# Seven-product matrix multiplication: another order of the seven products, and another split of the weight sums between transfer and VectorE

## The chip, the cores and the metric

The kernel runs on one core of one Trainium2 chip. The metric is the device time of one execution in microseconds (us). In the rows PE is TensorE's matmul, PEld its weight load, DVE is VectorE, ACT is ScalarE, POOL is GpSimd, and SP (SPq) is the queue of SyncE, which issues most of the transfers (DMA). An instruction runs on its engine in the order in which the program lists it; engines wait for one another by semaphores.

## The reference, cut to what matters

The reference is one block of a diffusion model on 512 tokens of width 2048: a mixer (a state-space scan beside a long convolution), then a SwiGLU feed-forward layer of width 5632, all in float32. The change touches the feed-forward layer alone:

```python
def swiglu(h, wg, wu, wd):
    return (jax.nn.silu(h @ wg) * (h @ wu)) @ wd
...
        x = x + g2 * rmsnorm(swiglu(h, w_gate[layer], w_up[layer], w_down[layer]), norm_ffn_post[layer])
```

## The kernel before, in words

**Arithmetic.** Each float32 operand is held as a rounded high part and a low part (`whi`, `wlo` for weights; `fh`, `fl` and `th`, `tl` for activations), and a product is three matmuls: high by high (line 1433), high weight by low activation (1435), low weight by high activation (1436).

**Groups and places.** Most of the feed-forward layer is done in 54 groups (`quad(q)`), 38 of `w_gate` and `w_up` in turn (even numbers are `w_gate`), then 16 of `w_down`. A group multiplies a 2 by 2 arrangement of weight blocks W11, W12, W21, W22 (`r11`, `r12`, `r21`, `r22`, each 128x1024, 512 KB, all named `rq` in the rows) by a 2 by 2 arrangement of activation blocks with seven block products instead of eight (Winograd's form of Strassen's method). Below, a *place* is the position of a product in its group, 1 to 7; the code counts `i` from 0. A place is 8 steps of three matmuls of 256 columns. Of the seven weight operands four are sums of blocks: W21+W22 is always made by a transfer that adds into its destination (`accum_op=ADD`, issued by POOL) during the group before; of the others, before, W11+W21 is made by such a transfer within the group, into `r11`, and the two that build on it, W11+W21+W22 in `r22` and the sum of all four in `r12`, by DVE. The activation operands (blocks in `fh`/`fl`, sums in `th`/`tl`) stay in place for 38 groups, and are replaced twice, at groups 38 and 46, when `w_down` needs the next part of the hidden layer (`replace`): transfers from `hd` into `tl` and `fl`, then a cast on ACT (line 1368) and a subtraction on DVE (1370) for each.

**What sets the order.** `feed(raw, body)` is called once for each place, in order. It issues the cast of the high part on ACT (1347) and, one call later, the subtraction for the low part on DVE (line 80, by `pend`); the matmuls of a place are issued two calls after its own. `late` holds a group's result sums, `hooks` the actions of a numbered call (`at(n, ...)`): the transfers and splits of `replace`, and `sums`, which makes the sums `T` of a finished hidden block. Instructions of one engine may be moved past each other by a scheduler before the program is fixed, except DMA issues and the splits of `replace`, which are pinned. The result `R` of a group collects the products from four accumulators in PSUM (`acc`, one bank each, two products in most). `ada(1)` is a piece of another, small computation: it loads a 512 KB block into the buffer `T` (`rt<-in_ada`) and adds it into `ada` with two DVE operations (line 77), in `w_gate` groups and in some of `w_down`. `KICKS` splits one matmul of a group in two narrower ones, at a place that runs through a cycle of six groups; the rows below use these split matmuls, which show as `x2`, as marks of a place.

Of the kernel before, what the change touches and what calls it, by code (L numbers as in the profile page):

```python
# [65 lines left out]
def block_kernel(ctx: ExitStack, tc: tile.TileContext, I: dict, out: bass.AP, dbg=None, stop=None):  # L66
    nc = tc.nc
# [1259 lines left out]
    def place(j, k, area):  # L1327
        if j == 0:
            return [f[:, area : area + 256] for f in fx[k]]
        if j in (1, 6):  # L1330
            o = 0 if j == 1 else 256
            return [f[:, o : o + 256] for f in fx[k + 8]]
        b = {2: 3, 3: 0, 4: 2, 5: 1}[j]
        return [t[:, b, :] for t in tx[k]]

    SRC = {0: 0, 1: 2, 6: 3, 3: 4, 5: 5, 4: 6, 2: 7}
# [35 lines left out]
    def replace(q, c, area):  # L1372

        n = 7 * (q - 1)
        for j, load, first in ((1, 4, 6), (6, 9, 11)):
            for k in range(8):
                d = place(j, k, 0)
                at(n + load, lambda d=d, k=k, j=j: op_load(d, hd[CH[c][k]][:, SRC[j], :]))
                at(n + first + k // 2, lambda d=d: op_split(d))
        for o, loads, first in ((2, (7, 5), 9), (0, (6, 8), 10)):  # L1380
            for k in range(8):
                for e in range(2):
                    d = [t[:, o + e, :] for t in tx[k]]
                    at(n + loads[e], lambda d=d, k=k, e=e, o=o: op_load(d, hd[CH[c][k]][:, 4 + o + e, :]))
                d = [t[:, o : o + 2, :] for t in tx[k]]
                at(n + first + k // 4, lambda d=d: op_split(d))
        for k in range(8):
            d = place(0, k, area)
            at(7 * (q - 4) + k, lambda d=d, k=k: op_load(d, hd[CH[c][k]][:, 0, :]))
            at(7 * (q - 4) + k + 2, lambda d=d: op_split(d))  # L1390
# [22 lines left out]
    nxt = [qload(t, quads[0][0][i, j]) for t, i, j in (("ra", 0, 0), ("ra", 0, 1), ("raw", 1, 0), ("raw", 1, 1))]  # L1413
    dma(nxt[2], quads[0][0][1, 1], nc.gpsimd, accum_op=ADD)

    def quad(q):
# [5 lines left out]
        def body(i):  # L1422
            def run(w):
                if i in (0, 2, 3, 5):
                    ps[i] = acc()
                b, o = {0: (0, 0), 1: (0, 1), 2: (2, 1), 3: (3, 1), 4: (3, 0), 5: (5, 0), 6: (2, 0)}[i]
# [17 lines left out]
        def early():  # L1444
            p12, p75, p6 = ps[0], ps[3], ps[5]
            nc.scalar.copy(out=R[:, 0, :], in_=p12[:, 0:256])
            tt(nc.vector, R[:, 0, :], p6[:, 0:256], R[:, 0, :], SUB)
            tt(nc.vector, R[:, 2, :], R[:, 0, :], p75[:, 0:256], SUB)
            tt(nc.vector, R[:, 1:4:2, :], R[:, 0:4:2, :], p75[:, 256:512].unsqueeze(1).broadcast_to([128, 2, 256]), ADD)
            nc.scalar.copy(out=R[:, 0, :], in_=p12[:, 0:256])  # L1450
            tt(nc.vector, R[:, 0, :], R[:, 0, :], p12[:, 256:512], ADD)

        def end():

            tt(nc.vector, R[:, 1, :], ps[2][:, 0:256], R[:, 1, :], SUB)
            tt(nc.vector, R[:, 2, :], R[:, 2, :], ps[2][:, 256:512], SUB)
# [21 lines left out]
        nsrc = quads[q + 1][0] if more else None  # L1478
        n11 = qload("ra", nsrc[0, 0] if more else I["w_dc"][2])
        feed(r11, body(0))  # L1480
        n12 = qload("ra", nsrc[0, 1] if more else I["w_dc"][3])
        n21 = qload("raw", nsrc[1, 0] if more else I["w_dc"][0])
        feed(r12, body(1))
        dma(r11, src[1, 0], nc.gpsimd, accum_op=ADD)
        if more:
            dma(n21, nsrc[1, 1], nc.gpsimd, accum_op=ADD)
        feed(r22, body(2))
        feed(r21, body(3))
        feed(r11, body(4))
        if kind != "w_up" and q < NG + 10:  # L1490
            ada(1)
        tt(nc.vector, r22, r22, r11, ADD)
        n22 = qload("raw", nsrc[1, 1] if more else I["w_dc"][1])
        feed(r22, body(5))
        tt(nc.vector, r12, r12, r22, ADD)
        feed(r12, body(6))
# [279 lines left out]
```

## Time and profile before

| | before |
|---|---|
| median of 3 runs | 2528.96 us (2522.35 to 2530.49) |
| the profiled execution | 2524.72 us, of which its span is 2523.0 us |
| granted TensorE clock, mean over the span | 0.975 |
| PE busy | 2390.1 us (95% of the span) |
| DVE busy | 1888.3 us (75%) |
| ACT busy | 972.0 us (39%) |
| POOL busy | 558.9 us (22%) |

The page of the profile gives busy time by engine, the chain of waits that ended last, and groups of like instructions. Since matmuls overlap in their pipeline, a busy PE is not a PE at its best pace; the pace is read from start to start of marked matmuls. The groups run from 1274.19 us to about 2366 us of the span. Times in rows are us from the start of the span.

### The profile page before, as it was taken

How to read it: one execution, taken by the hardware profiler on the slowest of the kernel's cores; microseconds unless marked ns; L12 is line 12 of the kernel's file. 1: busy time of each engine (PE TensorE's matmuls, PEld its weight loads, DVE VectorE, ACT ScalarE, POOL GpSimd, SP SyncE). 2: the span in 40 equal slices, each digit the busy share in tenths (PEclk: the TensorE clock that was granted, in tenths of full speed). 3: DMA queues.
4: the chain of work that ended last, by engine and by line, in shares of the span. 5: the costliest groups of instructions: out<-in, count | busy, mean ns of one | idle time of the engine just before them, and what ended most of it. 6: DMA issues, size and time to landing. Idle time of an engine off the chain costs nothing.

```text
span 2523.0 us, 41024 instructions
## 1 busy us (share of the span) xinstructions
PE 2390.1 (95%) x16138; PEld 2125.1 (84%) x16138; DVE 1888.3 (75%) x2478; ACT 972.0 (39%) x1351; POOL 558.9 (22%) x537
## 2 busy tenths in 40 slices
PE   8999999899899999998999999999999989999996
PEld 3467879677666788998999999999999989989986
DVE  7986756788878866688967777777777788677546
ACT  3143325222123412455434444444444454444334
POOL 1230010466523334653010000000000000000105
PEclk9999999999899999999999999999999989989998
DMA  7867754444455575646677676767777788777853
GB/s 290 304 228 243 236 170 157 158 134 159 146 186 185 186 283 177 208 142 194 192 208 205 193 210 194 192 193 200 218 203 194 218 243 237 225 204 196 247 179 127
DMA packets 183593, 508.72 MB, mean 202 GB/s; under 512 B 19455, under 2 KB 65471, under 8 KB 181864
## 3 DMA queue, kind: packets, MB, share of 16 engines
q1 hardware_dynamic: 166696, 445.27, 52.1%
q0 software_dynamic: 16704, 60.82, 13.7%
q8 instruction: 127, 2.08, 0.3%
q14 instruction: 66, 0.54, 0.1%
HBM read 454.12 MB, written 51.90 MB: 201 GB/s over the span
## 4 chain that ended last, share of the span: by engine, by line
PE 42%; DVE 6%; DMA 5%; issue 2%; ACT 1%; POOL 1%; SPq 0%; POOLq 0%; DVEq 0%; ACTq 0%
PE acc L1433 12%; PE acc L1436 12%; PE acc L1435 12%; PE acc L83 5%; DVE wlo L80 2%; DMA rq<-in_w_up 2%; DMA rq<-in_w_gate 1%; DVE y L80 1%; DMA fl<-hd 1%; DMA tl<-hd 1%; DVE tb L80 0%; POOL gs L80 0%; DMA hd<-sg 0%; DMA raw<-in_w_up 0%; ACT whi L1347 0%
## 5 line engine op out<-in xcount | busy, mean ns | idle before, releaser
L1347 ACT CAST whi<-rq 128x1024 fp32r<-128x1024 f32 x378 | 397.3, 1051 | 568.7 <-PE acc L1435 442.9
L80 DVE TENSOR_TENSOR wlo<-rq,whi 128x1024 fp32r<-128x1024 f32 x382 | 464.6, 1222 | 150.5 <-ACT whi L1347 144.8
L1433 PE MATMUL acc<-th,whi 128*128 128x256 f32 (+1 forms) x1755 | 486.3, 280 | 13.0 <-ACT th L1368 9.6
L1436 PE MATMUL acc<-th,wlo 128*128 128x256 f32 x1728 | 484.3, 280 | 11.6 <-DVE wlo L80 11.6
L1435 PE MATMUL acc<-tl,whi 128*128 128x256 f32 x1728 | 485.4, 281 | 2.0 <-DVE tl L1370 1.4
L179 ACT CAST whi<-raw 128x1024 fp32r<-128x1024 f32 (+1 forms) x216 | 221.5, 1026 | 481.6 <-PE acc L83 276.1
L1433 PE MATMUL acc<-fh,whi 128*128 128x256 f32 (+1 forms) x1323 | 361.5, 276 | 1.9 <-ACT whi L1347 1.3
L1435 PE MATMUL acc<-fl,whi 128*128 128x256 f32 x1296 | 359.2, 277 | 0.0
L1436 PE MATMUL acc<-fh,wlo 128*128 128x256 f32 x1296 | 358.7, 277 | 0.0
L80 DVE TENSOR_TENSOR wlo<-raw,whi 128x1024 fp32r<-128x1024 f32 x200 | 260.7, 1303 | 123.6 <-ACT whi L179 119.9
L1433 PEld LDWEIGHTS acc<-th,whi 128*128 128x128 f32 x1755 | 332.3, 191 | 14.8 <-ACT th L1368 13.1
L1436 PEld LDWEIGHTS acc<-th,wlo 128*128 128x128 f32 x1728 | 329.4, 191 | 13.7 <-DVE wlo L80 13.5
L1435 PEld LDWEIGHTS acc<-tl,whi 128*128 128x128 f32 x1728 | 329.8, 191 | 4.4 <-DVE tl L1370 4.3
L83 PE MATMUL acc<-hh,whi 128*128 128x512 f32 x688 | 285.1, 416 | 3.9 <-ACT hh L74 3.7
L83 PE MATMUL acc<-hl,whi 128*128 128x512 f32 x688 | 277.4, 403 | 3.6 <-DVE hl L77 3.6
L83 PE MATMUL acc<-hh,wlo 128*128 128x512 f32 x688 | 276.6, 402 | 0.0
L1433 PEld LDWEIGHTS acc<-fh,whi 128*128 128x128 f32 x1323 | 246.4, 188 | 2.6 <-ACT whi L1347 1.5
L1435 PEld LDWEIGHTS acc<-fl,whi 128*128 128x128 f32 x1296 | 244.0, 188 | 0.0
L1436 PEld LDWEIGHTS acc<-fh,wlo 128*128 128x128 f32 x1296 | 243.4, 188 | 0.0
L77 DVE SCALAR_TENSOR_TENSOR ada<-raw,cc,ada 128x512 f32<-128x512 f32 x198 | 169.5, 856 | 42.1 <-DMA raw<-in_ada 39.6
L80 DVE TENSOR_TENSOR rq<-rq,rq 128x1024 f32<-128x1024 f32 x108 | 132.1, 1223 | 66.2 <-DMA rq<-in_w_up 42.2
L83 PEld LDWEIGHTS acc<-hh,whi 128*128 128x128 f32 x688 | 134.3, 196 | 39.6 <-issue 5.6
(333 smaller groups left out, 4523.7 us busy)
## 6 DMA issues: line engine op xcount, KB each, us to landing
raw<-in_ada SPq DMA_DIRECT2D x106, 512.0 KB, 4.0
rq<-in_w_gate SPq DMA_DIRECT2D x76, 512.0 KB, 5.7
rq<-in_w_up SPq DMA_DIRECT2D x76, 512.0 KB, 4.3
ada<-in_ada SPq DMA_DIRECT2D x64, 512.0 KB, 4.7
rq<-in_w_ds SPq DMA_DIRECT2D x64, 512.0 KB, 4.3
raw<-in_w_hy SPq DMA_DIRECT2D x44, 512.0 KB, 3.8
raw<-in_w_out SPq DMA_DIRECT2D x41, 512.0 KB, 3.8
raw<-in_w_xbc SPq DMA_DIRECT2D x38, 512.0 KB, 3.9
```

The source lines that it names most:

```text
L77: nc.vector.scalar_tensor_tensor(out=o, in0=a, scalar=s, in1=b, op0=op0, op1=op1)
L80: e.tensor_tensor(out=o, in0=a, in1=b, op=op)
L83: nc.tensor.matmul(o, lhsT, rhs, start=start, stop=stop)
L179: nc.scalar.copy(out=hi[:, :n], in_=raw[:, :n])
L1347: nc.scalar.copy(out=hi, in_=raw)
L1433: nc.tensor.matmul(p[:, c0:c1], wh, xh[:, c0:c1], start=k == 0 and c0 == 0, stop=False, skip_group_check=True)
L1435: nc.tensor.matmul(p, wh, xl, start=False, stop=False, skip_group_check=True)
L1436: nc.tensor.matmul(p, wl, xh, start=False, stop=k == 7, skip_group_check=True)
```

## The change

The products keep their operands and change their places: before the order was p1 p2 p3 p4 p5 p6 p7 in the code's own numbering (`i` = 0 to 6); now it is p1, the product of W21+W22, that of W12, that of W22, that of W11+W21+W22, that of all four, and at the seventh place that of W11+W21. DVE now makes the sums for places 5 and 6, `r21 += r11` and `r12 += r21`, from blocks that are there early, and the transfer that adds W21 into `r11` serves the seventh place. W21+W22, made by a transfer in the group before, is used at place 2 instead of 4. `R` is formed by one ACT copy instead of two and by six DVE operations as before; the products of places 5 and 7 now share a PSUM bank, where before those of places 3 and 7 did, and the product of place 6 had one alone. The loads of the next group's blocks come in the order W12, W11, W21, W22. `ada(1)` is called after the load of the next W22. In `replace` the activations change their slots: 8 splits of 512 columns and 32 of 256 now, 16 and 16 before, for each exchange (those of place 1 apart).

```diff
--- before.py
+++ after.py
@@ -1327,13 +1327,13 @@
     def place(j, k, area):
         if j == 0:
             return [f[:, area : area + 256] for f in fx[k]]
-        if j in (1, 6):
-            o = 0 if j == 1 else 256
+        if j in (2, 5):
+            o = 0 if j == 2 else 256
             return [f[:, o : o + 256] for f in fx[k + 8]]
-        b = {2: 3, 3: 0, 4: 2, 5: 1}[j]
+        b = {1: 0, 3: 3, 4: 1, 6: 2}[j]
         return [t[:, b, :] for t in tx[k]]
 
-    SRC = {0: 0, 1: 2, 6: 3, 3: 4, 5: 5, 4: 6, 2: 7}
+    SRC = {0: 0, 2: 2, 5: 3, 1: 4, 4: 5, 6: 6, 3: 7}
 
     late, pend = [], []
     step, hooks = [0], {}
@@ -1372,18 +1372,17 @@
     def replace(q, c, area):
 
         n = 7 * (q - 1)
-        for j, load, first in ((1, 4, 6), (6, 9, 11)):
+        for j, load, first in ((1, 4, 6), (2, 5, 7), (5, 8, 10), (6, 9, 11)):
             for k in range(8):
                 d = place(j, k, 0)
                 at(n + load, lambda d=d, k=k, j=j: op_load(d, hd[CH[c][k]][:, SRC[j], :]))
                 at(n + first + k // 2, lambda d=d: op_split(d))
-        for o, loads, first in ((2, (7, 5), 9), (0, (6, 8), 10)):
-            for k in range(8):
-                for e in range(2):
-                    d = [t[:, o + e, :] for t in tx[k]]
-                    at(n + loads[e], lambda d=d, k=k, e=e, o=o: op_load(d, hd[CH[c][k]][:, 4 + o + e, :]))
-                d = [t[:, o : o + 2, :] for t in tx[k]]
-                at(n + first + k // 4, lambda d=d: op_split(d))
+        for k in range(8):
+            for j, load in ((3, 6), (4, 7)):
+                d = place(j, k, 0)
+                at(n + load, lambda d=d, k=k, j=j: op_load(d, hd[CH[c][k]][:, SRC[j], :]))
+            d = [t[:, 1:4:2, :] for t in tx[k]]
+            at(n + 10 + k // 4, lambda d=d: op_split(d))
         for k in range(8):
             d = place(0, k, area)
             at(7 * (q - 4) + k, lambda d=d, k=k: op_load(d, hd[CH[c][k]][:, 0, :]))
@@ -1410,7 +1409,8 @@
         return raw
 
     ada_raw[0] = raw_t
-    nxt = [qload(t, quads[0][0][i, j]) for t, i, j in (("ra", 0, 0), ("ra", 0, 1), ("raw", 1, 0), ("raw", 1, 1))]
+    nxt = [qload(t, quads[0][0][i, j]) for t, i, j in (("ra", 0, 1), ("ra", 0, 0), ("raw", 1, 0), ("raw", 1, 1))]
+    nxt[0:2] = nxt[1::-1]
     dma(nxt[2], quads[0][0][1, 1], nc.gpsimd, accum_op=ADD)
 
     def quad(q):
@@ -1421,9 +1421,9 @@
 
         def body(i):
             def run(w):
-                if i in (0, 2, 3, 5):
+                if i in (0, 1, 3, 4):
                     ps[i] = acc()
-                b, o = {0: (0, 0), 1: (0, 1), 2: (2, 1), 3: (3, 1), 4: (3, 0), 5: (5, 0), 6: (2, 0)}[i]
+                b, o = {0: (0, 0), 2: (0, 1), 1: (1, 0), 3: (3, 1), 5: (3, 0), 4: (4, 0), 6: (4, 1)}[i]
                 p = ps[b][:, o * 256 : o * 256 + 256]
                 for k in range(8):
                     xh, xl = place(i, k, area)
@@ -1442,18 +1442,17 @@
             return run
 
         def early():
-            p12, p75, p6 = ps[0], ps[3], ps[5]
+            p12, p5, p34, p6 = ps[0], ps[1], ps[3], ps[4]
             nc.scalar.copy(out=R[:, 0, :], in_=p12[:, 0:256])
-            tt(nc.vector, R[:, 0, :], p6[:, 0:256], R[:, 0, :], SUB)
-            tt(nc.vector, R[:, 2, :], R[:, 0, :], p75[:, 0:256], SUB)
-            tt(nc.vector, R[:, 1:4:2, :], R[:, 0:4:2, :], p75[:, 256:512].unsqueeze(1).broadcast_to([128, 2, 256]), ADD)
-            nc.scalar.copy(out=R[:, 0, :], in_=p12[:, 0:256])
+            tt(nc.vector, R[:, 2, :], p6[:, 0:256], R[:, 0, :], SUB)
             tt(nc.vector, R[:, 0, :], R[:, 0, :], p12[:, 256:512], ADD)
+            tt(nc.vector, R[:, 3, :], R[:, 2, :], p5[:, 0:256], ADD)
+            tt(nc.vector, R[:, 1, :], p34[:, 0:256], R[:, 3, :], SUB)
+            tt(nc.vector, R[:, 2, :], R[:, 2, :], p34[:, 256:512], SUB)
 
         def end():
 
-            tt(nc.vector, R[:, 1, :], ps[2][:, 0:256], R[:, 1, :], SUB)
-            tt(nc.vector, R[:, 2, :], R[:, 2, :], ps[2][:, 256:512], SUB)
+            tt(nc.vector, R[:, 2:4, :], R[:, 2:4, :], ps[4][:, 256:512].unsqueeze(1).broadcast_to([128, 2, 256]), SUB)
             if kind == "w_gate":
                 act(R, R, AF.Silu)
                 gate[m] = R
@@ -1476,24 +1475,24 @@
         r11, r12, r21, r22 = nxt
         more = q + 1 < len(quads)
         nsrc = quads[q + 1][0] if more else None
+        n12 = qload("ra", nsrc[0, 1] if more else I["w_dc"][3])
+        feed(r11, body(0))
         n11 = qload("ra", nsrc[0, 0] if more else I["w_dc"][2])
-        feed(r11, body(0))
-        n12 = qload("ra", nsrc[0, 1] if more else I["w_dc"][3])
+        feed(r21, body(1))
         n21 = qload("raw", nsrc[1, 0] if more else I["w_dc"][0])
-        feed(r12, body(1))
+        feed(r12, body(2))
+        tt(nc.vector, r21, r21, r11, ADD)
         dma(r11, src[1, 0], nc.gpsimd, accum_op=ADD)
+        feed(r22, body(3))
+        tt(nc.vector, r12, r12, r21, ADD)
         if more:
             dma(n21, nsrc[1, 1], nc.gpsimd, accum_op=ADD)
-        feed(r22, body(2))
-        feed(r21, body(3))
-        feed(r11, body(4))
+        feed(r21, body(4))
+        feed(r12, body(5))
+        n22 = qload("raw", nsrc[1, 1] if more else I["w_dc"][1])
         if kind != "w_up" and q < NG + 10:
             ada(1)
-        tt(nc.vector, r22, r22, r11, ADD)
-        n22 = qload("raw", nsrc[1, 1] if more else I["w_dc"][1])
-        feed(r22, body(5))
-        tt(nc.vector, r12, r12, r22, ADD)
-        feed(r12, body(6))
+        feed(r11, body(6))
         nxt[:] = [n11, n12, n21, n22]
 
     replace(NG, 0, 256)
```

How instructions move is shown at three places of the same `w_gate` group in the middle of the run.

DVE, from the low part of place 3 (before) and of place 2 (now) on. In the rows of before `rq_12430`, `rq_12461`, `rq_12463` and `rq_12591` are r11, r12, r21 and r22 of the group; `R_12429` is the result of the group before:

```order
L80 TENSOR_TENSOR wlo_12725<-rq_12591,whi_12724 128x1024
L80 TENSOR_TENSOR R_12429<-R_12429,acc_12508 128x256
L80 TENSOR_TENSOR rq_12591<-rq_12591,rq_12430 128x1024
L80 TENSOR_TENSOR R_12429<-R_12429,R_12196 128x1024
L80 TENSOR_TENSOR wlo_12758<-rq_12463,whi_12757 128x1024
L80 TENSOR_TENSOR T_12786<-R_12429 128x2x256
L80 TENSOR_TENSOR rq_12461<-rq_12461,rq_12591 128x1024
L80 TENSOR_TENSOR T_12786<-R_12429,T_12786 128x256
L80 TENSOR_TENSOR wlo_12792<-rq_12430,whi_12791 128x1024
L80 TENSOR_TENSOR T_12786<-T_12786,R_12429 128x256
L80 TENSOR_TENSOR wlo_12828<-rq_12591,whi_12827 128x1024
```

and now, where `rq_12455`, `rq_12425`, `rq_12491` and `rq_12615` are r11, r12, r21 and r22, and `R_12424` the result of the group before:

```order
L80 TENSOR_TENSOR wlo_12680<-rq_12491,whi_12679 128x1024
L80 TENSOR_TENSOR rq_12491<-rq_12491,rq_12455 128x1024
L80 TENSOR_TENSOR R_12424<-R_12424,acc_12621 128x512
L80 TENSOR_TENSOR wlo_12716<-rq_12425,whi_12715 128x1024
L80 TENSOR_TENSOR R_12424<-R_12424,R_12192 128x1024
L80 TENSOR_TENSOR rq_12425<-rq_12425,rq_12491 128x1024
L80 TENSOR_TENSOR T_12779<-R_12424 128x2x256
L80 TENSOR_TENSOR wlo_12750<-rq_12615,whi_12749 128x1024
L80 TENSOR_TENSOR T_12779<-R_12424,T_12779 128x256
L80 TENSOR_TENSOR T_12779<-T_12779,R_12424 128x256
L80 TENSOR_TENSOR wlo_12787<-rq_12491,whi_12786 128x1024
```

Before, the sum `rq_12591 += rq_12430` reads r11 after the transfer has added into it, and stands ahead of the low part of place 4 (`wlo_12758`). Now the first sum follows the low part of place 2 and reads no block that a transfer of this group has added into.

SP, from the store of that result to the next loads. Before:

```order
L163 DMA hd<-R_12429 128x1024
L163 DMA hd<-T_12786 128x1024
L163 DMA rt_12820<-in_ada 128x1024
L163 DMA rq_12825<-in_w_up 128x1024
L163 DMA rq_12886<-in_w_gate 128x1024
```

and now:

```order
L163 DMA hd<-R_12424 128x1024
L163 DMA hd<-T_12779 128x1024
L163 DMA rq_12843<-in_w_up 128x1024
L163 DMA rt_12845<-in_ada 128x1024
L163 DMA rq_12879<-in_w_gate 128x1024
```

The load of the next W22 (the first `rq`) has moved ahead of the load for `ada` (`rt`), whose buffer is the one that `T` is stored from.

PE, the last two matmuls of place 6 and the first of place 7, with what they wait for. Before:

```order
L1435 MATMUL acc_12892<-tl_10468,whi_12827 128x256
L1436 MATMUL acc_12892<-th_10467,wlo_12828 128x256
L1433 MATMUL acc_12795<-fh_9053,whi_12857 128x256 [waits Activation_49]
L1435 MATMUL acc_12795<-fl_9054,whi_12857 128x256
L1436 MATMUL acc_12795<-fh_9053,wlo_12858 128x256 [waits DVE_49]
```

and now:

```order
L1435 MATMUL acc_12818<-fl_9096,whi_12814 128x256
L1436 MATMUL acc_12818<-fh_9095,wlo_12815 128x256
L1433 MATMUL acc_12853<-th_10077,whi_12849 128x256 [waits DVE_49,Activation_49]
L1435 MATMUL acc_12853<-tl_10078,whi_12849 128x256
L1436 MATMUL acc_12853<-th_10077,wlo_12850 128x256
```

The first matmul of place 7 now also waits for DVE: it writes the bank (`acc_12853`) in which the product of place 5 lies until DVE has read it for `R`.

## Rows read from the trace of the kernel before

**Rows 1.** Windows: stretch, length; busy PE, PEld, DVE, ACT, POOL; clock, DMA share, GB/s.
```profile
1292.00:2025.00 733.00, 726.13 (x6336) 723.85 (x6335) 557.82 (x675) 317.92 (x367) 66.11 (x75) 1.00 0.73 201
2025.00:2061.00 36.00, 25.60 (x170) 23.44 (x169) 28.69 (x45) 19.55 (x38) 1.76 (x2) 0.81 0.82 257
...
2195.00:2232.00 37.00, 28.87 (x180) 26.47 (x179) 28.00 (x47) 20.50 (x38) 2.65 (x3) 0.77 0.80 241
```

**Rows 2.** Timeline of PE, marks: start, duration, shapes; count x2 where split.
```profile
1274.19 0.39 PE L1433 MATMUL acc<-fh,whi 128*128 128x16 f32 x2
...
1307.07 0.36 PE L1433 MATMUL acc<-th,whi 128*128 128x64 f32 x2
...
1751.49 0.39 PE L1433 MATMUL acc<-fh,whi 128*128 128x16 f32 x2
...
1792.54 0.38 PE L1433 MATMUL acc<-fh,whi 128*128 128x32 f32 x2
...
2013.05 0.36 PE L1433 MATMUL acc<-th,whi 128*128 128x64 f32 x2
2026.78 0.38 PE L1433 MATMUL acc<-fh,whi 128*128 128x32 f32 x2
...
2071.17 0.33 PE L1433 MATMUL acc<-th,whi 128*128 128x128 f32 x2
...
2187.05 0.33 PE L1433 MATMUL acc<-th,whi 128*128 128x128 f32 x2
...
2231.33 0.35 PE L1433 MATMUL acc<-fh,whi 128*128 128x96 f32 x2
```

**Rows 3.** Waits of PE from 1292 to 2025 us: total, times, longest.
```profile
PE acc L1436 <- DVE wlo L80: 6.3, 8, 1.4
PE acc L1433 <- DVE R L80: 0.6, 3, 0.2
```

**Rows 4.** Chain of waits: start, us, what.
```profile
1523.34 0.78 PE aux L83 x8
...
1806.36 8.92 DMA rq<-in_w_up
```

**Rows 5.** Timeline of DVE in the same stretch; in brackets the idle time before.
```profile
1815.37 1.23 DVE L80 TENSOR_TENSOR rq<-rq,rq 128x1024 f32<-128x1024 f32 x1 [3.02 <-DMA rq<-in_w_up]
```

**Rows 6.** Timeline of POOL, ACT and PE in the first group.
```profile
1271.48 1.98 POOL L163 DMA_DIRECT2D rq<-in_w_gate  x2 [101.59 <-DMA rq<-in_w_up]
...
1279.29 1.05 ACT L1347 CAST whi<-rq 128x1024 fp32r<-128x1024 f32 x1 [3.96 <-DMA rq<-in_w_gate]
...
1285.89 0.45 PE L1436 MATMUL acc<-th,wlo 128*128 128x256 f32 x1 [3.02 <-DVE wlo L80]
```

**Rows 7.** Timeline of ACT in the first exchange of activations.
```profile
2031.48 2.18 ACT L1368 CAST th<-tl 128x512 fp32r<-128x512 f32 x4 [4.79 <-DMA tl<-hd]
...
2045.72 0.71 ACT L1368 CAST fh<-fl 128x256 fp32r<-128x256 f32 x2 [4.11 <-DMA fl<-hd]
```

**Rows 8.** Timeline of SP and DVE in group 26, a `w_gate` group.
```profile
1799.77 0.33 SPq L163 DMA_DIRECT2D hd<-T  x1
1802.36 0.33 SPq L163 DMA_DIRECT2D rt<-in_ada  x1
...
1805.97 1.54 DVE L77 SCALAR_TENSOR_TENSOR ada<-rt,cc,ada 128x512 f32<-128x512 f32 x2
```

**Rows 9.** The tile rt from 1270 to 2300 us: its loads, issue to landing.
```profile
L163 SPq DMA_DIRECT2D rt<-in_ada x22: 333/333/937, 1275.2 to 2122.8; - x22
...
DMA to landing us min/median/max: 3.4/3.6/8.3
```

**Rows 10.** Groups of like DVE instructions from 1292 to 2025 us, shapes apart.
```profile
L80 DVE TENSOR_TENSOR wlo<-rq,whi 128x1024 fp32r<-128x1024 f32 x262 | 318.2, 1222 | 96.0 <-ACT whi L1347 92.7
L80 DVE TENSOR_TENSOR R<-acc,R 128x256 f32<-128x256 f32 x76 | 32.2, 423 | 16.0 <-PE acc L1436 11.5 <-DMA rq<-in_w_up 0.5
```

**Rows 11.** DMA issues by POOL from 1300 to 2000 us: count, size, median us to landing.
```profile
rq<-in_w_up POOLq DMA_DIRECT2D x35, 512.0 KB, 7.0
```

## The prediction

> **What bounds the kernel now.** I read the windows first. From 1292 to 2025 us, the bulk of the `w_gate` and `w_up` groups, PE is busy 726.13 of 733 us at a granted clock of 1.00, that is at the upper of its two levels, 2.4 GHz, while DVE is busy 558 us and the DMA engines 0.73 of the time [rows 1]. So PE sets the pace there, and only what stops PE can be won. In the two stretches with an exchange of activations PE is busy 25.6 of 36 us and 28.9 of 37 us, at clocks of 0.81 and 0.77 [rows 1].
>
> How much is lost is read from the marks. Between the marks at 1751.49 (place 1 of group 24) and 1792.54 (place 2 of group 26) lie 15 places without a stop: 41.05 / 15 = 2.74 us a place, 19.2 us a group [rows 2]. Against this pace:
> - from 1307.07 to 2013.05 (place 4 of groups 1 and 37) 252 places took 705.98 us where 252 x 2.737 = 689.7 are due: 16.3 us too much. Two sets of eight small matmuls of the `ada` computation lie among them, 0.78 us each [rows 4], so 14.7 us are stops and what follows from them;
> - from 1274.19 to 1307.07 ten places took 32.9 us instead of 27.4: 5.5 us at the start;
> - from 2026.78 to 2071.17 and from 2187.05 to 2231.33 ten places took 44.4 and 44.3 us: 17.0 and 16.9 us in the exchanges [all rows 2].
>
> What the stops are, the waits of PE say: 6.3 us in 8 waits for `wlo`, 0.6 us in 3 waits for `R` [rows 3]. (These 6.9 us are idle time; the marks count also the slower matmuls at and after each stop.) The chain of waits shows where `wlo` comes from: at 1806.36 POOL issues the transfer that adds W21 into `r11`, and it takes 8.92 us [rows 4]. DVE stands idle for 3.02 us until 1815.37 for it, at the sum `r22 += r11` [rows 5], which stands ahead of the low part of place 4 in DVE's queue. So a transfer wanted at place 5 stops place 4. At the median of 7.0 us [rows 11] it is in time, at 9 to 10 us it is not.
>
> **The change part by part.**
>
> *The stops in the groups.* No sum on DVE reads a transferred block of its own group any more. The transfer into `r11` starts after `r21 += r11`: the low part of place 2 ends about 0.4 us before the group starts (its high part is cast as place 6 of the group before ends), the sum ends at 0.75 us, and the transfer, at 7.0 to 10 us, lands 8 to 11 us after the start. The cast for place 7 is due, as every cast, two places ahead, at 4 x 2.74 = 11.0 us, and place 7 starts at 16.4 us: even 10 us leave some 3 us after a cast (1.05 us [rows 6]) and a low part (1.22 us [rows 10]). W21+W22, wanted two places sooner than before, is added by a transfer issued behind that one, about 2 us into the group before; it lands by 12 us there, and its cast is due at 16.4. The three waits for `R` go too: the bank that place 1 of the next group needs is released after two DVE operations that wait for the product of place 5, not of place 6. Of the 14.7 us I leave 1.5 us as an estimate for transfers that are later still: -13.2 us. Bounds: -14.7, and 0 if other stops take their place.
>
> *The new wait at place 7.* Places 5 and 7 share a bank, so place 7 waits for the DVE operation that reads the product of place 5. That operation stands behind the two `ada` operations on DVE, and those wait for the load `rt`, which stands behind the next W22 on SP and needs the buffer that `T` is stored from. In group 26, which starts at 1792.54 - 2.74 = 1789.80, `T` was stored at 1799.77, `rt` issued 2.6 us later, and `ada` ran at 1805.97, 3.6 us after that [rows 8]. Now DVE has after the group's start: the sum to 0.75, the last operation on `R` (0.65), a low part, the product with the gate and a sum (1.14 each, start to start), `T` (0.6, 0.35, 0.35) and a low part (1.14): store at about 7.3, `rt` at 10.0, landed at 13.6 with the median of 3.6 us [rows 9], `ada` done at 15.1 (1.54 us [rows 8], less overlap), the read at 15.5 (0.42 us [rows 10]). Place 7 starts at 16.4: 0.9 us to spare. 22 groups have such a load [rows 9], the first in group 0 with no stored `T` ahead of it; of the 21 others some five are in `w_down`, where the low part of place 7 also stands behind `ada` and the margin is about nil. Bounds: nothing at 3.6 us, and at the largest landing of 8.3 us [rows 9] 13.6 + 4.7 + 1.9 - 16.4 = 3.8 us in each of 21 groups, 80 us. I take the median, since 8.3 us belongs to a `w_down` group in which other loads were under way, and 0.5 us in each of four `w_down` groups: +2 us.
>
> The Trainium skill bears on this: "PSUM — Partial Sum Buffer", section "PSUM bank collisions raise a hardware error", says that two engines must not touch one bank in the same partitions at a time, at whatever columns, so that accesses are to be ordered by bank. No run here shows a collision; by that rule the sharing has to cost a wait, which is what the order of the matmuls shows.
>
> *The exchanges.* The same bytes are moved. ACT stood idle for 4.79 us until 2031.48 for the first joint split, which needed the slots of two places, and for 4.11 us until 2045.72 for the first split of the last slot [rows 7]; the other splits stand behind it in ACT's queue. Now the second and third product find their activations split singly and run on, but the joint split for places 4 and 5 stands behind the first of place 6, and half of it behind the first of place 7. So the stop still ends when the first load of the last slot lands. After 2045.72 the group needed 14.5 us (group 39 starts at 2071.17 - 4 x 2.74 = 2060.2 [rows 2]) for about 3.5 places, 9.6 us. Of these 4.9 us some went to sums that DVE made late; now they are made early. I take 1.5 us off in each exchange: -3 us. Eight more splits on ACT and DVE in each lie in time in which those engines wait for loads; without that cover they cost about 1.3 us each. Bounds for both together: -14 (nothing lost before the last slot lands) and +11 (two more places held in each, 4 x 2.74).
>
> *The start.* The transfer for W21+W22 is issued at 1271.48 and landed at 1279.29; PE waited 3.02 us for `wlo` [rows 6], at place 4, behind both transfers. Now place 2 needs the first of them. It is due at 1274.19 + 2.74 = 1276.9, and its low part can be ready at 1279.3 + 1.05 + 1.2 = 1281.5: a wait of some 4.4 us in place of 3.0. The second transfer is no longer beside it, which may give some back: +0.8 us, from -2 to +3.
>
> *Nothing else:* one ACT copy less and six DVE operations on `R` as before lie beside PE's work.
>
> **The sum.** -13.2 + 2 - 3 + 0.8 = -13.4 us, against the profiled execution of 2524.7 us: 2511.3 us. That execution lies 4 us below the median of the runs shown, inside their 2522 to 2530; I put the median at 2512.
>
> **The rivals.**
>
> *The stops are only moved (no change).* PE at 99% leaves every lateness visible, and the transfers are as many and as long. If in each of the 36 groups 0.4 us came back, at place 2 for W21+W22 or at place 7 for the last sum, the 14.7 us would be used up: about 2524. For it speaks that the first group already shows the wait at place 2; against it the margin of about 3 us at both places. Half of that with exchanges 5 us worse gives about 2523 as well.
>
> *Slower: place 7 waits for the `ada` load.* The mechanism is the queue above: W22's load, then `rt`, then `ada`, then the read, then PE. It decides from a landing of 4.5 us after issue. With 6 us each of 21 groups stops for 1.5 us, 32 us in all: 2511 + 32 - 2 = 2541. For it speaks that the load now follows another by 1.5 us and that `w_down` groups had up to 8.3 us; against it the median of 3.6 us and a load that no longer waits until 12.6 us into the group.
>
> *More is won.* If the exchanges lose only what the last slot's landing dictates, they give 14 us instead of 3: 2500.
>
> **How the numbers follow.** Forecast 0.58, only moved 0.24, slower 0.10, more won 0.08. A measurement of this kernel can tell about 0.3%, 7.6 us. The forecast's own range, 2503 to 2519, lies nearly all beyond it: faster 0.58 - 0.02 + 0.08 = 0.64; within 0.3% 0.26; slower 0.10. The range that holds 8 in 10 goes from 2500, the end of the last case, to 2528, the end of "no change", and leaves out the slower case and the tails.
>
> **What would show it.** Right: from mark to mark 36 groups at 19.2 us each, no wait of PE for `wlo` between 1292 and 2025 us, and no idle DVE ahead of an `rq` sum. A wait of PE for `R` at 16.4 us into a group would show the new wait, with `ada` just before it on DVE. In the exchanges ACT should stand idle once, long, ahead of the split for place 6. The forecast is wrong if PE's lost time from 1307 to the first exchange is over 5 us, or an exchange loses over 20 us.

## The result: slower, and where the profile shows the time

| | before | changed |
|---|---|---|
| median of 4 runs each | 2529.57 us | 2586.58 us (2582.07 to 2595.87) |
| ratio | 1 | 1.0231, 95% interval 1.0209 to 1.0253 |
| the profiled execution, its span | 2524.7, 2523.0 us | 2583.3, 2581.5 us |
| mark to mark, place 4 of group 1 to place 4 of group 37 | 705.98 us | 741.72 us |

The time forecast was 2512 us, in a range of 2500 to 2528. The changed kernel takes 57 us more than the kernel before.

The windows of the changed kernel answer to [rows 1] (stretch, length; busy PE, PEld, DVE, ACT, POOL; clock, DMA share, GB/s):

```profile
1292.00:2025.00 733.00, 698.49 (x6027) 695.57 (x6026) 534.13 (x644) 291.21 (x310) 62.99 (x71) 0.99 0.67 191
2061.00:2110.00 49.00, 38.03 (x257) 36.86 (x258) 41.45 (x72) 24.66 (x47) 3.53 (x4) 0.79 0.84 244
```

(The second window is that of the first exchange.) In the bulk PE is idle for 34.5 us where it was for 6.9. No engine has become the bound: DVE is busy for 534 us instead of 558, and the mean DMA share has fallen, because the same work is spread over a longer time. (A mean over 733 us hides short stretches in which the DMA engines are full; e6 comes to one.)

The marks, answering to [rows 2]:

```profile
1308.83 0.36 PE L1433 MATMUL acc<-th,whi 128*128 128x64 f32 x2
...
1864.05 0.37 PE L1433 MATMUL acc<-fh,whi 128*128 128x48 f32 x2
...
1882.00 0.35 PE L1433 MATMUL acc<-fh,whi 128*128 128x96 f32 x2
...
2050.55 0.36 PE L1433 MATMUL acc<-th,whi 128*128 128x64 f32 x2
2070.99 0.38 PE L1433 MATMUL acc<-th,whi 128*128 128x32 f32 x2
2113.72 0.33 PE L1433 MATMUL acc<-th,whi 128*128 128x128 f32 x2
```

From place 4 of group 1 to place 4 of group 37 are 741.72 us, 50.4 us more than the 689.7 + 1.6 that are due there; before it was 14.7. From place 3 of group 28 (1864.05) to place 1 of group 29 (1882.00) five places took 17.95 us instead of 13.72. The same happens, with 1.6 to 5.4 us, between the marks of 15 of the `w_gate` groups; between two marks that hold only `w_up` places at most 0.7 us are lost.

The waits of PE say what it stops for. From 1292 to 2025 us, answering to [rows 3], and from 2025 to 2440 us:

```profile
PE acc L1433 <- DVE R L80: 33.7, 15, 3.6
PE acc L1436 <- DVE wlo L80: 0.8, 1, 0.8
```

```profile
PE acc L1433 <- DVE R L80: 22.5, 8, 4.6
```

The waits for `wlo` that the change was to remove are gone (6.3 us in 8 waits before, 0.8 in one now), and DVE hardly stands idle any more ahead of a sum of blocks (1.8 us in the bulk, 55.0 before). In their place PE waits for `R`. It is place 7, at its first matmul, as group 28 shows. Its place 3 is marked at 1864.05, so it starts at 1864.05 - 2 x 2.744 = 1858.56. POOL, SP, DVE and PE in it, one fence each:

```profile
1860.19 0.88 POOL L163 DMA_DIRECT2D rq<-in_w_gate  x1 [16.22 <-DVE R L80]
1860.79 1.18 POOL L163 DMA_DIRECT2D rq<-in_w_up  x1
```

```profile
1862.45 0.33 SPq L163 DMA_DIRECT2D hd<-R  x1
1866.12 0.33 SPq L163 DMA_DIRECT2D hd<-T  x1
1866.55 1.26 SPq L163 DMA_DIRECT2D rq<-in_w_up  x1
1872.12 0.33 SPq L163 DMA_DIRECT2D rt<-in_ada  x1
```

```profile
1875.67 1.54 DVE L77 SCALAR_TENSOR_TENSOR ada<-rt,cc,ada 128x512 f32<-128x512 f32 x2 [3.66 <-DMA rt<-in_ada]
1877.13 0.42 DVE L80 TENSOR_TENSOR R<-acc,R 128x256 f32<-128x256 f32 x1
```

```profile
1877.69 0.55 PE L1433 MATMUL acc<-th,whi 128*128 128x256 f32 x1 [2.47 <-DVE R L80]
...
1878.26 0.41 PE L1436 MATMUL acc<-th,wlo 128*128 128x256 f32 x1
1878.47 0.41 PE L1433 MATMUL acc<-th,whi 128*128 128x256 f32 x1
```

Read backwards: PE waits 2.47 us for the operation on `R` that reads place 5, that stands on DVE behind `ada`, DVE waits 3.66 us for the load `rt`, and the load was issued 6.0 us after the store of `T`. In group 26 of the kernel before it was 2.6 us [rows 8].

The stop costs more than its idle time. The matmuls after it start 0.21 us apart (1878.26 to 1878.47), not 0.114, for 16 matmuls; the granted clock of that stretch is at the lower of the two levels, 1.2 GHz:

```profile
1877.60:1881.00 3.40, 3.31 (x16) 3.34 (x17) 3.30 (x6) 0.00 (x0) 0.00 (x0) 0.52 0.38 155
```

16 x 0.1 = 1.6 us, and 2.6 us of stop (start to start, less the pace; 2.47 of it are idle): the 4.2 us between the marks.

**Where the 58.5 us of the span are**, all from the marks against the undisturbed pace, changed less before (the pace is 2.744 us a place here and below, 13.72 us for five places without a stop; by the prediction's 2.737 ten places come out 0.07 us larger): the 36 groups +35.7; groups 37 to 38, ahead of the first exchange, +6.7; the ten places of the first exchange 15.3 instead of 17.0, -1.7; between the exchanges +10.0; the second exchange with the places ahead of it 20.9 instead of 16.8, +4.1; the last groups -0.7; the start of the groups -0.2; ahead of the first mark +1.9 and behind the last +2.6.

Of the experiments below, e4 had a disturbed profiled execution (6408 us): nothing is read from its trace, and its ratio leaves it out.

### The profile page after: what moved, and what is told of

Read it like the earlier page. It is cut to its first block, busy times and chain, and to the rows that moved or that the text cites. A ratio compares the mean times of both kernels' runs of the same rounds, so it can differ in the third digit from the quotient of the medians.

```text
span 2581.5 us, 40974 instructions
## 1 busy us (share of the span) xinstructions
PE 2403.5 (93%) x16138; PEld 2140.3 (83%) x16138; DVE 1890.6 (73%) x2494; ACT 957.1 (37%) x1313; POOL 559.7 (22%) x537
## 5 line engine op out<-in xcount | busy, mean ns | idle before, releaser
L1433 PE MATMUL acc<-th,whi 128*128 128x256 f32 (+1 forms) x1755 | 493.0, 284 | 63.5 <-DVE R L80 56.2
L1433 PEld LDWEIGHTS acc<-th,whi 128*128 128x128 f32 x1755 | 337.8, 194 | 68.4 <-issue 28.2
L1433 PE MATMUL acc<-fh,whi 128*128 128x256 f32 (+2 forms) x1323 | 361.7, 277 | 0.1
L1436 PEld LDWEIGHTS acc<-th,wlo 128*128 128x128 f32 x1728 | 335.1, 194 | 6.1 <-DVE wlo L80 6.1
L1435 PEld LDWEIGHTS acc<-tl,whi 128*128 128x128 f32 x1728 | 335.1, 194 | 1.8 <-DVE tl L1370 1.8
L77 DVE SCALAR_TENSOR_TENSOR ada<-raw,cc,ada 128x512 f32<-128x512 f32 x198 | 169.2, 855 | 41.2 <-DMA raw<-in_ada 38.7
L83 PE MATMUL acc<-fh,wlo 128*128 128x256 f32 (+1 forms) x512 | 158.2, 310 | 7.7 <-DVE wlo L80 7.7
```

Source lines behind the costliest of these rows:

```text
L77: nc.vector.scalar_tensor_tensor(out=o, in0=a, scalar=s, in1=b, op0=op0, op1=op1)
L83: nc.tensor.matmul(o, lhsT, rhs, start=start, stop=stop)
L1433: nc.tensor.matmul(p[:, c0:c1], wh, xh[:, c0:c1], start=k == 0 and c0 == 0, stop=False, skip_group_check=True)
L1435: nc.tensor.matmul(p, wh, xl, start=False, stop=False, skip_group_check=True)
L1436: nc.tensor.matmul(p, wl, xh, start=False, stop=k == 7, skip_group_check=True)
```

## The experiments

Eleven kernels ran, in three sets (e1 to e4; e5 to e8; e9 to e11), each on a chip of its own. Ratios are to the kernel before, run on the same chip; the marks are those of one profiled execution of each kernel.

| run | median us | ratio (95%) | mark to mark, groups 1 to 37 |
|---|---|---|---|
| before | 2529 to 2533 | 1 | 705.98 |
| changed | 2586.6 | 1.0231 (1.0209, 1.0253) | 741.72 |
| e1_ada_first | 2579.5 | 1.0202 (1.0178, 1.0227) | 729.98 |
| e2_own_bank | 2560.1 | 1.0123 (1.0102, 1.0145) | 721.89 |
| e3_before_ada_late | 2529.1 | 1.0010 (0.9995, 1.0025) | 701.69 |
| e4_both | 2550.5 | 1.0093 (1.0074, 1.0112) | - |
| e5_ada_in_up | 2548.2 | 1.0063 (1.0048, 1.0078) | 703.05 |
| e6_sum_first | 2567.7 | 1.0145 (1.0130, 1.0160) | 713.45 |
| e8_up_and_bank | 2535.8 | 1.0029 (1.0017, 1.0042) | 697.12 |
| e7_none_in_down | 2525.9 | 0.9979 (0.9967, 0.9992) | 696.48 |
| e9_before_ada_moved | 2532.1 | 1.0002 (0.9986, 1.0019) | 713.22 |
| e10_sum_first | 2528.3 | 0.9990 (0.9976, 1.0004) | 695.28 |
| e11_late_splits | 2527.5 | 0.9985 (0.9970, 1.0001) | 700.89 |

My first theory (A) had the chain as read above and held that the store of `T` is late because the load of W22 now follows it on SP. The rivals: the new order leaves DVE no room whatever the load does (B), and `rt` itself lands slowly (C).

### e1: the load for ada ahead of W22's again

```diff
-        n22 = qload("raw", nsrc[1, 1] if more else I["w_dc"][1])
         if kind != "w_up" and q < NG + 10:
             ada(1)
+        n22 = qload("raw", nsrc[1, 1] if more else I["w_dc"][1])
```

> The changed kernel with two lines exchanged: `ada(1)` stands ahead of the load of the next W22 again, so only the order of two loads on SP differs. Theory A (the load for ada is late because the store of T now lands beside W22's load, 5.2 us instead of 2.6, and the read of place 5 stands behind ada on DVE): T's store lands in 2.6 us again, rt is issued at about 10.2 us into a w_gate group, ada ends at about 15.4, the wait for R at place 7 is gone from nearly all w_gate groups, from place 4 of group 1 to place 4 of group 37 about 695 us (741.7 in the changed kernel), and the time is 2510 to 2530 us. Rival B (the new order of the products itself, with its earlier sums and two products in the bank of places 5 and 7, leaves DVE no room whatever the load does): the stops stay, 2560 to 2590. Rival C (the load rt itself lands slowly among the others, whichever store is ahead): half the stops stay, about 2550.

Measured: 2579.5 us, 7 us less than the changed kernel (the intervals of the two overlap), and far from 2510 to 2530. From 1292 to 2025 us PE waits:

```profile
PE acc L1433 <- DVE R L80: 26.5, 15, 2.7
```

DMA issues from 1300 to 2000 us in the same run (count, size, median us to landing):

```profile
hd<-T SPq DMA_DIRECT2D x16, 512.0 KB, 5.6
rt<-in_ada SPq DMA_DIRECT2D x15, 512.0 KB, 3.6
```

The store of `T` still takes 5.6 us with no load of W22 beside it. So the load on SP is not what makes it late, and `rt` itself lands in 3.6 us as before: theory C falls, and of A the part on the order of the two loads. B stands.

### e2: a bank alone for place 7

```diff
-                if i in (0, 1, 3, 4):
+                if i in (0, 1, 3, 6):
-                b, o = {0: (0, 0), 2: (0, 1), 1: (1, 0), 3: (3, 1), 5: (3, 0), 4: (4, 0), 6: (4, 1)}[i]
+                b, o = {0: (0, 0), 2: (0, 1), 1: (1, 0), 3: (3, 1), 5: (3, 0), 4: (1, 1), 6: (6, 0)}[i]
```

(with the six operations of `early` and `end` reading the new places)

> The changed kernel with other banks: place 5 shares the bank of place 2, and place 7 has one alone; the order on every engine is that of the changed kernel. Theory A: place 7 no longer waits for R. What is late is now place 1 of the next group, whose bank is released behind ada, the read of place 5, a low part and one more sum on DVE: due 2.74 us later than place 7, released about 1.5 us later, so about 1 us of each 2.3 us stop is left. Time about 2555 us (2540 to 2570), and the waits of PE for R stand at place 1, not at 7. If the bank had no part in it (rival: the low parts behind ada are what PE lacks): the same waits turn up for wlo, and the time stays at 2575 to 2590.

Measured: 2560.1 us, as expected of A. The waits stand where it put them, at place 1 of the next group and about 1 us long. The waits of PE from 1292 to 2025 us, and one stop, at a mark of place 1:

```profile
PE acc L1433 <- DVE R L80: 11.6, 12, 2.1
```

```profile
1386.07 0.42 PE L1433 MATMUL acc<-fh,whi 128*128 128x96 f32 x2 [0.83 <-DVE R L80]
```

So the shared bank is what turns DVE's lateness into a stop of place 7; the lateness itself is still there.

### e3: the kernel before, with ada called after W22's load

```diff
-        if kind != "w_up" and q < NG + 10:
-            ada(1)
         tt(nc.vector, r22, r22, r11, ADD)
         n22 = qload("raw", nsrc[1, 1] if more else I["w_dc"][1])
+        if kind != "w_up" and q < NG + 10:
+            ada(1)
```

> The kernel before with one edit: `ada(1)` is called after the load of the next W22, as in the changed kernel; products, sums and banks are those of before. Theory A: rt becomes as late as in the changed kernel (the store of T lands in about 5 us), DVE waits for it, but there no place waits for a read that stands behind ada within its own group; only place 1 of the next group can, for a bank released behind ada. Time 2530 to 2550. If the late load alone were enough: as the changed kernel, about 2575 to 2590. If the order of the two loads does not matter: 2527 to 2532.

Measured: 2529.1 us, no difference: the last of the three expectations. The store of `T` among the DMA issues from 1300 to 2000 us:

```profile
hd<-T SPq DMA_DIRECT2D x16, 512.0 KB, 3.1
```

A load of W22 behind the store of `T` makes the store 0.5 us slower than in the kernel before (2.6 us), where the changed kernel has it 2.6 us slower. The same edit, taken out of the changed kernel (e1) and put into the kernel before (e3), does little in both: the late store has another cause.

### e4: the edits of e1 and e2 together

> The changed kernel with both edits: ada's load ahead of W22's, and a bank alone for place 7. Theory A: no wait for R within the groups; what the forecast wanted, about 2512 us (2505 to 2522). Rival B: the early sums or the exchanges cost by themselves, no faster than the kernel before, 2528 or more.

Measured: 2550.5 us, about what the two gains add up to (2586.6 - 7 - 26.5 = 2553), not 2512. That is the range of rival B; theory A missed.

### e5: ada in the w_up groups

```diff
-        if kind != "w_up" and q < NG + 10:
+        if kind != "w_gate" and q < NG + 10:
             ada(1)
```

> The changed kernel with one word changed: `ada(1)` is called in w_up groups (and w_down) instead of w_gate groups (and w_down). In a w_up group no T is stored, so the load rt waits for no store. Theory A, as the first four runs left it (place 7 stops because the read of place 5 stands behind ada on DVE, ada waits for rt, rt for the store of T, and that store is late beside other transfers, whatever the order of the two loads): the 15 stops of the w_gate groups go, 742 us from mark to mark become about 695, and the time falls by about 45 to 2540 us (2530 to 2550); what is lost in the w_down groups stays. Rival B (the w_gate groups are too full for DVE with the new sums, and place 7 is late without ada too): the waits for R stay at half or more, 2560 or above.

Measured: 2548.2 us, within what was expected of A; 703.05 us from mark to mark, where 695 were expected. From 1292 to 2025 us:

```profile
PE acc L1433 <- DVE R L80: 7.5, 4, 3.1
```

With the same products, sums and banks, 11 of 15 stops are gone once no `ada` stands ahead of the read, and 38.7 us from mark to mark with them; B, which wanted half of the waits to stay, falls for these groups. The store of `T` is as late as ever here (5.9 us), only nobody waits for it in the group.

### e6: the transfer for W21+W22 ahead of the one into r11

```diff
         n21 = qload("raw", nsrc[1, 0] if more else I["w_dc"][0])
+        if more:
+            dma(n21, nsrc[1, 1], nc.gpsimd, accum_op=ADD)
...
-        if more:
-            dma(n21, nsrc[1, 1], nc.gpsimd, accum_op=ADD)
```

Theory D, formed after e1 and e3, names the cause of the late stores. In group 26 of the kernel before, which starts at 1789.80, POOL issued its two adding transfers 2.6 and 0.3 us ahead of the group's start and SP stored `R` 5.3 us after it. POOL and SP there:

```profile
1787.18 0.89 POOL L163 DMA_DIRECT2D rq<-in_w_gate  x1 [10.38 <-DVE wlo L80]
1789.51 0.88 POOL L163 DMA_DIRECT2D rq<-in_w_up  x1 [1.44 <-DMA rq<-in_w_up]
```

```profile
1795.09 0.33 SPq L163 DMA_DIRECT2D hd<-R  x1
1799.77 0.33 SPq L163 DMA_DIRECT2D hd<-T  x1
```

In group 28 of the changed kernel (above) both start 1.6 and 2.2 us after it, behind DVE's first sum, and the stores of `R` at 3.9 and of `T` at 7.6 us fall among them.

> The changed kernel with the transfer that adds W22 into the next group's W21 called right after that block's load, and so ahead of the transfer into r11 on POOL, as it does not stand behind DVE's first sum. Theory D (the stores of R and T are late, 7.6 and 5.2 us instead of 2.6 and 2.6, because both adding transfers now start about 2 us into the group, where before they had started at -2.6 and -0.3 us): with one of them done earlier R lands in 4 to 5 us, T in 3 to 4, rt is issued about 2 us earlier, the stops at place 7 fall to a third, and the time to 2555 to 2570 us. If the stores are late for another reason (the two transfers of SP beside them): they stay at 7.6 and 5.2, and the time at 2580 to 2590.

Measured: 2567.7 us, within what D expected. POOL now issues the one transfer at the start of the group (in group 28, which starts at 1841.00, at 1841.05), the other 1.6 us after it, and the stores follow (DMA issues from 1300 to 2000 us in this run, then in the changed kernel, then in the kernel before; the waits of PE from 1292 to 2025 us in this run):

```profile
hd<-R SPq DMA_DIRECT2D x17, 512.0 KB, 5.4
hd<-T SPq DMA_DIRECT2D x16, 512.0 KB, 3.9
```

```profile
hd<-R SPq DMA_DIRECT2D x17, 512.0 KB, 7.6
hd<-T SPq DMA_DIRECT2D x16, 512.0 KB, 5.2
rt<-in_ada SPq DMA_DIRECT2D x15, 512.0 KB, 3.9
```

```profile
hd<-R SPq DMA_DIRECT2D x18, 512.0 KB, 2.6
hd<-T SPq DMA_DIRECT2D x16, 512.0 KB, 2.6
```

```profile
PE acc L1433 <- DVE R L80: 18.4, 13, 6.4
```

The stops fell from 33.7 to 18.4 us, to a little over a half, where D expected a third.

How the transfers delay the stores can be read from the DMA engines themselves. Here are the queues behind the issue of the store of `R`: in group 26 of the kernel before, 1795.1 to 1797.7, and in group 28 of the changed kernel, 1862.5 to 1865.0 and then 1865.5 to 1868.0 (packets, MB, share of the 16 engines; a packet counts where it starts, so a little over 100% can come out; q0 has POOL's transfers, q1 those of SP):

```profile
q1 hardware_dynamic: 144, 0.52, 49.3%
```

```profile
q0 software_dynamic: 135, 0.49, 107.8%
```

```profile
q0 software_dynamic: 86, 0.35, 70.5%
q1 hardware_dynamic: 76, 0.31, 32.9%
```

Before, the engines carry the store alone and have time to spare; in the changed kernel they are full with POOL's two transfers, and nothing of the store moves. Counted over all 17 stores of `R` from 1300 to 2000 us, the first packet of SP's queue starts 2.8 us after the issue (median; 0.8 in the kernel before), with no other queue than POOL's at work until then, and POOL's last packet ends 6.9 us after the issue, in e6 4.1. A packet of 4 KB takes 0.33 us in an adding transfer and 0.16 us in one of SP (medians), so two adding transfers of 128 such packets fill 16 engines for 2 x 128 x 0.33 / 16 = 5.3 us. The store of `T`, 3.7 us behind that of `R`, then meets the rest of both: in the 2.6 us behind its issue POOL's queue takes 0.63 of the engines and SP's 0.42, where before it was nothing and 0.51. So theory D is shown, for `R` by POOL's transfers alone, for `T` by them and by the store of `R` that they have held up.

The start and the first exchange lost 5 to 6 us more each (11.1 and 20.5 us instead of 5.3 and 15.3), the second with the places ahead of it 0.5; that the transfer into `r11` stands on POOL there behind one that waits for its block is a likely reason, which no run shows.

### e8 and e7: both edits, and no ada in w_down

e8 is e5 with the banks of e2. e7 is e8 with

```diff
+        if kind == "w_up" and q >= 19:
+            ada(1)
         feed(r12, body(2))
...
-        if kind != "w_gate" and q < NG + 10:
+        if kind == "w_up":
             ada(1)
```

> `ada(1)` in w_up groups and a bank alone for place 7, together. Theory A: the stops of the w_gate groups go by the first edit; in the w_down groups, where place 7 waits for a read behind splits or ada, the second takes away some 10 to 15 us: 2520 to 2530 us, about the kernel before or a little faster. Rival B: not under 2545.

> As the run with both edits, and `ada(1)` is called twice in the last ten w_up groups and not in w_down, so that no load of it meets the replacements. Theory A: no wait for rt anywhere near a replacement; the forecast's own 2512 us at best, 2508 to 2525. If what is lost in w_down is the new order of splits and not ada: no faster than the run with both edits.

Measured: 2535.8 us for e8, 6 us over the range expected; from 2025 to 2440 us the waits for `R` are nearly gone (1.7 us in 2 waits, 20.7 in 7 in e5), but 16.9 us in 14 waits for `wlo` stand there, some of them behind `ada`. e7 takes away those between the exchanges (9.9 us in 9 waits are left, nearly all about the exchanges): 2525.9 us, 0.9 us over the range expected, and 0.21% less than the kernel before (interval 0.08% to 0.33%). From 1292 to 2025 us PE waits:

```profile
PE acc L1436 <- DVE wlo L80: 3.3, 5, 1.3
PE acc L1433 <- ACT whi L1347: 0.7, 1, 0.7
```

From mark to mark it takes 696.5 us, 5 us over what is due.

### e9: the control

The kernel before with `ada(1)` moved as in e7, and nothing else:

```diff
+        if kind == "w_up" and q >= 19:
+            ada(1)
         feed(r22, body(2))
...
-        if kind != "w_up" and q < NG + 10:
+        if kind == "w_up":
             ada(1)
```

> A control: the kernel before with `ada(1)` moved as in the run without ada in w_down (in w_up groups, twice in the last ten), and nothing else. If the gain of that run over the kernel before (2525.9 against 2529.7) comes from the new order of products, this one keeps the waits for wlo at place 4 behind late transfers into r11, loses some 10 to 15 us from mark to mark, and stays within 2526 to 2533. If it comes from where ada stands, this one is as fast or faster, 2522 to 2526, and the new order is worth nothing.

Measured: 2532.1 us, ratio 1.0002; the waits for `wlo` are back (all that PE waits for from 1292 to 2025 us):

```profile
PE acc L1436 <- DVE wlo L80: 13.5, 10, 3.0
```

713.2 us from mark to mark against 696.5 in e7: with `ada` in the same place, the new order takes 16.7 us less there in these two executions. How far one execution can be trusted is seen from the others: the three with the old order (before, e3, e9) took 701.7 to 713.2 us, the four with the new order and neither the shared bank nor `ada` in the `w_gate` groups (e7, e8, e10, e11) 695.3 to 700.9. The new order is the faster in every pair, by anything from 1 to 18 us. Of the whole time little of it is left: the intervals of e7 and e9 overlap.

### e10 and e11: two more edits of e7

e10 calls the transfer for W21+W22 as e6 does, from the third group on (`q >= 2`). e11 calls the splits for places 2 and 3 of an exchange two calls later, four at a time:

```diff
-                at(n + first + k // 2, lambda d=d: op_split(d))
+                at(n + (first + 2 + k // 4 if j < 3 else first + k // 2), lambda d=d: op_split(d))
```

> The run without ada in w_down and with a bank alone for place 7, and now the transfer for W21+W22 is called ahead of the one into r11, from the third group on. Theory D: the store of R lands in about 5.4 us instead of 7.6 here too, but nothing waits for that store any more, so the groups gain at most the 5 us that they still lose from mark to mark: 2521 to 2527 us. Rival: the transfer into r11, now behind the other one on POOL, comes late for place 7 and at the replacements, where its block is loaded late (the replacements lost 5 us more each in the run that had this edit alone): 2530 to 2540.

> The run without ada in w_down and with a bank alone for place 7, and the splits for places 2 and 3 of a replacement are called two calls later and four at a time. They stand on ACT ahead of the casts of the last places of the group before, and wait there for their loads; 3.6 us are lost before each replacement (marks of groups 38 and 46), which the kernel before did not lose at 38 (0.0). If it is that, 3 to 6 us come back: 2519 to 2523 us. If the splits themselves are then late for places 2 and 3: no gain or a loss, 2525 to 2532.

Measured: 2528.3 and 2527.5 us, neither to be told apart from e7. In e10 the store of `R` lands in 6.7 us, where D expected 5.4 and e7 has 7.6. (In e6 only the first exchange had lost 5 us more, not each, as the text above has it.) The groups gain 1.2 us, and the second exchange with the places ahead of it loses 20.5 us instead of 14.9. In e11 the 3.6 us ahead of each exchange are gone (0.0 at the marks of groups 38 and 46), and the places behind lose as much more: 17.0 and 16.3 us, 33.3 in both exchanges; e7 loses 33.4 in all, the kernel before 33.8. The loss is only moved. That what an exchange loses is set by its loads, whatever the order, would fit this; no run took a load away.

## Why the prediction was wrong, point by point

**The step that failed is the new wait at place 7, in one link: from the store of `T` to the issue of `rt`, taken as 2.6 us and measured as 6.0.** The queue was named rightly (W22's load, `rt`, `ada`, the read, PE), and so was where it ends. Group 28 of the changed kernel against the forecast, in us from the group's start:

| | forecast | measured |
|---|---|---|
| `T` stored | 7.3 | 7.6 |
| `rt` issued | 10.0 | 13.6 |
| `rt` landed, `ada` starts | 13.6 | 17.1 |
| `ada` done | 15.1 | 18.6 |
| read of place 5 done | 15.5 | 19.0 |
| place 7 starts | 16.4 | 19.1 |

Every link but one has its forecast length. From the store of `T` to the issue of `rt` I took the 2.6 us of [rows 8], where nothing else was under way, and put no bounds on them; the bounds I gave were those of the landing of `rt`, which stayed at a median of 3.9 us. And the same text moves both adding transfers to about 2 us after the group's start: it prices when they land, and not what they do to the two stores that start among them. That they delay the stores is shown by e6 (one of them earlier gave back 2.2 of 5.0 us for `R` and 1.3 of 2.6 for `T`) and by the DMA engines, which they fill for the first 2.8 us behind the issue of `R`. The Trainium skill, "DMA: Bandwidth & Descriptors", section "Queues, rings and completion order", says that each DMA engine takes turns between the queues that have work for it, and drains a whole packet (there a group of descriptors) from one before it switches. The trace agrees in part: from 1865.5 to 1868.0 both queues get through, but ahead of that POOL's alone did; whether that was one such group, no run here shows. The mean DMA share of the groups, 0.73 before and 0.67 now, hides it.

So the term of +2 us is in truth some 48 us in the 36 groups (50.4 us lost there, of which 1.5 were forecast for other reasons), and about 20 us more in w_down and ahead of the exchanges. The rival "place 7 waits for the `ada` load" was the case that came about, but with 1.5 us a group, decided by the landing of `rt`; measured were 2.25 us of idle time a stop (33.7 / 15) and about 3 with the slower matmuls behind it. Two conditions had to meet, and the runs tell them apart: the bank (e2: -26 us) and `ada` ahead of the read behind a late store (e5: -38 us). The order of the two loads on SP, to which the prediction gave a place in the chain, is worth some 7 us at most (e1, not clear of noise).

**The stops in the groups: right in kind, somewhat less in size.** Forecast -13.2 us. The waits for `wlo` fell from 6.3 to 0.8 us in the changed kernel; freed of the other wait (e7) the groups take 9.5 us less from mark to mark than in the kernel before and 16.7 less than in the control, one execution of each. 1.5 us were left as later stops; it is 5.

**The exchanges: the sign only at one place.** Forecast -1.5 each. The ten marked places of the first lose 15.3 instead of 17.0, but the places ahead of it lose 6.7 us that they didn't: the splits for places 2 and 3 stand on ACT ahead of the cast for place 7 of the group before and wait for their loads. (With the bank and `ada` mended, in e7, 3.6 of the 6.7 us are left; e11 shows that these are the splits'.) ACT in group 37:

```profile
2056.65 0.71 ACT L1368 CAST th<-tl 128x256 fp32r<-128x256 f32 x2 [4.65 <-DMA tl<-hd]
2058.63 0.74 ACT L1368 CAST fh<-fl 128x256 fp32r<-128x256 f32 x2 [1.27 <-DMA fl<-hd]
2059.28 1.04 ACT L1347 CAST whi<-rq 128x1024 fp32r<-128x1024 f32 x1
```

I looked for stops within the exchange only. Counted with the places ahead, e7 loses 33.4 us in both and the kernel before 33.8: the term is about 0, not -3.

**The start: nearly nothing, within the bounds.** 5.26 us lost over ten places against 5.44, that is -0.2 where +0.8 was forecast. The wait is at place 2, as named (2.40 us for `whi` and 0.76 for `wlo`).

**Why e7 is not at 2512.** Its groups give 9.5 us and the exchanges 0.4, and its median is 3.8 us below that of the kernel before. In the two profiled executions the groups from the first mark to the last differ by 9.1 us (1063.8 against 1072.9), and the parts outside them take the rest back (first mark at 1279.3 instead of 1274.2; 179.8 instead of 175.9 behind the last). Between the profiled kernels the first mark varies from 1274.2 to 1285.5 us, so I can't say whether that belongs to the edits; it stays open.

## What to carry to other kernels

When a change moves a transfer, price it twice: when it lands, and what the stores and loads that it now overlaps do, with the chain that hangs on each; a landing time read from a stretch where the transfer was alone is a lower bound. A buffer shared by a store and a later load, an operation that waits for that load in the middle of a busy engine's queue, and a bank shared with a product that the same queue must read first are each harmless with time to spare, and together they stop the engine that sets the pace; take the waiting operation to where nothing hangs on it before tuning the order of loads.

## What was not expected of the hardware

A store of 512 KB that lands in 2.6 us alone took 7.6 us beside two adding transfers of the other queue, and 5.4 with one of them issued earlier. The mean DMA share of 0.67 hides the reason: just behind the issue of the store the engines are full, with 4 KB packets of the adding transfers that take 0.33 us each, twice the 0.16 us of plain ones. A stop of PE of 2.6 us was followed by 16 matmuls at the lower clock level (0.21 us apart, granted clock 0.52), which added 1.6 us. Not every stop is: the 15 stops cost 0.2 to 1.9 us beyond their idle time, 0.9 in the mean, by the marks around them.
